# RWKV's Gram masks: ScalarE copies and GpSimd selects, or bitwise AND on VectorE

## Chip, cores and metric

One Trainium2 chip, one of its cores, one program. The metric is the device time of one execution in microseconds (us), the median over several runs. The engines are called PE (TensorE, matmuls), DVE (VectorE), ACT (ScalarE), POOL (GpSimd) and SP (SyncE, which issues most weight loads).

## The reference, cut to what matters

One block over 256 tokens of width 2048: a normed input is projected, four branches (HGRN2, S5, RWKV-7, Mamba-2) each make a 1024-wide output, and the gated outputs are projected up, summed, projected and added to the input. The change lies in the RWKV branch, whose recurrence over tokens is

```python
def step(state, inp):
    r_t, w_t, k_t, v_t, kk_t, a_t = inp
    sa = jnp.einsum('bhvk,bhk->bhv', state, -kk_t)
    state = (state * w_t[:, :, None, :]
             + sa[..., None] * (kk_t * a_t)[:, :, None, :]
             + v_t[..., None] * k_t[:, :, None, :])
    return state, jnp.einsum('bhvk,bhk->bhv', state, r_t)
```

for 16 heads of 64 channels. The kernel computes it in 4 chunks of 64 tokens. Within a chunk, the products of every pair of tokens are needed for each head: a 64 x 64 Gram matrix of (b, k) against (r, -kk), of which only the part with the later token on one side counts. For the r columns the diagonal belongs to it, for the kk columns it does not. The rest must be zero: these are the masks.

## The kernel before

**The stream.** The large matmuls (the input projection, the up projections, the output projection) are cut into chunks of 512 KB of weights. For each chunk SP loads `raw`; ACT copies it to `hi` in a rounded format (`split`, L207); DVE subtracts to get `lo` (L216); PE multiplies `hi` and `lo` with the activations (`pg`, L261). There are 3 `raw` and 4 `hi`/`lo` buffers.

**The jobs.** The branches are generators, started as jobs with priorities, that issue a stage of instructions and yield. A planner keeps a modelled clock for each engine (`t_pe`, `t_act`, `t_dve`, `t_sw` for POOL) from cost formulas in the helpers: `act` books 0.06 us + 0.87 ns an element, `tt` (two-tensor DVE operations) 0.06 us + 1.045 ns an element, `select` and `ld` book on `t_sw`. Between chunks `run_jobs` issues stages as long as neither `t_dve` nor `t_act` is more than 3 us ahead of `t_pe`. So booked costs decide where in each engine's queue a stage lands; each engine then runs its queue in order. The RWKV job is `c` (priority 1); the Mamba job `d0` starts after it, then `d1`, `a0`, `a1`; S5 tiles run beside them at lower priority.

**The Gram stage** is in `rwkv_branch`, for chunks c = 0 to 3. Two groups `i4` of four head pairs: 8 matmuls of `bk` with `L1` fill two PSUM banks `ps[0]`, `ps[1]` (one for each head of a pair, `e`), 128 partitions by 4 x 128. Of each bank one half of the partitions (`x`) goes to the tile `GB`, the other half (`y`) back into the unused half of the tile `L1[c][e]`: four ACT copies of 64 x 512 for each group (L207), 32 in all. When both groups are there, POOL clears what the mask forbids, in place, with four selects of 64 x 1024 (`select`, L275), and loads one half of `GB` to memory as `dab` (`ld`, L280). Four PSUM banks are shared by all jobs (`wait_banks`); the next group's products need banks that the copies have emptied. For c < 3 the transposes of `bk` follow, which ACT copies to `bkT`.

**After it**, `dab` is read back as `XA`, an inverse is computed on DVE in 31 dependent steps (`invtmp`, `XT`), loaded out and back (`dtt`, `TT`), and the four chunks are run in order with `L1`, `GB`, `TT` and `bkT` on PE. The branch ends in `oc`, which is multiplied with a gate `zs` into the tiles `o`, the operand of the up projection.

**Setup.** `setup_consts` makes constants on POOL in the first 20 us, the mask tile `lmask` (used elsewhere) among them, with selects at L365 and L367.

Traces call the tiles by name without their numbers, so `L` is `L1` and `pb` any of the four shared PSUM banks.

Of the kernel before, what the change touches and what calls it, by code (L numbers as in the profile page):

```python
# [11 lines left out]
F32 = mybir.dt.float32  # L12
F32R = mybir.dt.float32r
I8 = mybir.dt.int8
BF16 = mybir.dt.bfloat16
AF = mybir.ActivationFunctionType
ALU = mybir.AluOpType
# [296 lines left out]
def setup_consts(K):  # L314
    nc = K.nc
    d = K.d
    c = K.const
    K.pt = c.tile([128, NPAR], F32, name="pt")
    src = {"norm_pre": d["norm_pre"], "lb": d["hgrn_lb_logits"], "hgrn_norm": d["hgrn_norm"],
           "s5_d": d["s5_d"], "b_glu": d["s5_b_glu"], "w0": d["rwkv_w0"], "a0": d["rwkv_a0"],  # L320
           "k_k": d["rwkv_k_k"], "k_a": d["rwkv_k_a"], "r_k": d["rwkv_r_k"], "ln_w": d["rwkv_ln_w"],
           "ln_b": d["rwkv_ln_b"], "m2_norm": d["m2_norm"], "conv_b": d["m2_conv_b"],
           "mu": d["rwkv_mu"], "conv_w": d["m2_conv_w"], "a_re": d["s5_a_re"], "a_im": d["s5_a_im"]}
    rows = K.big([128, 3, 128], name="prow")
    nc.vector.memset(rows, 0.0)
    for m, n in enumerate(_PAR_ROWS):
        if m in (6, 12):
            yield
        o, r = PAR[n]
        a = src[n][0]  # L330
        if len(a.shape) == 2:
            a = a.rearrange("a b -> (a b)")
        K.ldx(rows[o % 128:o % 128 + r, o // 128, :], a.rearrange("(r p) -> r p", p=128))
    yield
    K.ones = c.tile([128, 1], F32, name="ones")
    nc.gpsimd.memset(K.ones, 1.0)
    K.halfpi = c.tile([128, 1], F32, name="halfpi")
    nc.gpsimd.memset(K.halfpi, HALF_PI)

    K.ind = c.tile([128, 2, 32], F32, name="ind")  # L340
    nc.gpsimd.memset(K.ind, 0.0)
    for e in range(2):
        for g in range(2):
            nc.gpsimd.memset(K.ind[64 * e:64 * e + 64, g, 2 * g + e:2 * g + e + 1], 1.0)
    K.m64 = c.tile([128, 512], BF16, name="m64")
    nc.gpsimd.memset(K.m64, 1.0)
    nc.gpsimd.memset(K.m64[:, 0:512:64], 0.0)
    K.m256 = c.tile([128, 512], BF16, name="m256")
    nc.gpsimd.memset(K.m256, 1.0)
    nc.gpsimd.memset(K.m256[:, 0:512:256], 0.0)  # L350
    K.causal = c.tile([128, 128], F32, name="causal")
    nc.gpsimd.memset(K.causal, 1.0)
    nc.gpsimd.affine_select(out=K.causal, in_=K.causal, pattern=[[1, 128]], base=0, channel_multiplier=-1,
                            compare_op=ALU.is_ge, fill=0.0)

    K.lmask = c.tile([128, 7, 64], I8, name="lmask")
    nc.gpsimd.memset(K.lmask, 0.0)
    for e in range(2):
        x = slice(64 * e, 64 * e + 64)
        for lv in range(6):  # L360
            h = 1 << lv
            nb = 32 // h
            v = K.lmask[x, lv + 1, :].rearrange("p (b u) -> p b u", u=2 * h)[:, :, h:2 * h]
            nc.gpsimd.memset(v, 1.0)
            nc.gpsimd.affine_select(out=v, in_=v, pattern=[[-2 * h, nb], [0, h]], base=0, channel_multiplier=1,  # L365
                                    compare_op=ALU.is_ge, fill=0.0)
            nc.gpsimd.affine_select(out=v, in_=v, pattern=[[2 * h, nb], [0, h]], base=h - 1, channel_multiplier=-1,  # L367
                                    compare_op=ALU.is_ge, fill=0.0)
    K.omu = c.tile([128, 25], F32, name="omu")
    yield  # L370
    for e in range(2):
        x = slice(64 * e, 64 * e + 64)
        nc.vector.tensor_copy(out=K.lmask[x, 0, :], in_=K.ident[x, x])
    yield from K.wait_banks(1)
    ps = K.bank()
    for j in range(3):
        K.tr(ps[:, j * 128:(j + 1) * 128], rows[:, j, :])
    nc.vector.tensor_copy(out=K.pt, in_=ps[:, 0:NPAR])
    K.ts(K.omu, K.parv("mu"), -1.0, 1.0, ALU.mult, ALU.add)
# [16 lines left out]
def rwkv_branch(K, rw):  # L396

    nc = K.nc
# [10 lines left out]
    for g in range(2):  # L409
# [3 lines left out]
        for ii in range(4):  # L413
            i = 4 * g + ii
# [3 lines left out]
        for ii in range(4):  # L418
            i = 4 * g + ii
# [23 lines left out]
    ps = K.bank()  # L443
# [34 lines left out]
    ps = K.bank()  # L478
# [4 lines left out]
    b = ic  # L483
# [10 lines left out]
    L1 = [[K.big([128, 8, 2, 64], name=f"L1{c}{e}") for e in range(2)] for c in range(4)]  # L494
    for c in range(4):
        o = c % 2
        s0, s1 = 64 * c, 64 * c + 64
        for e in range(2):
            x = slice(64 * e, 64 * e + 64)
# [12 lines left out]
    for c in range(4):  # L512
# [3 lines left out]
        for e in range(2):  # L516
            x = slice(64 * e, 64 * e + 64)
# [9 lines left out]
    GB, bkT = [], []  # L527
# [3 lines left out]
    for c in range(4):  # L531
        o = c % 2
        GB.append(K.big([128, 8, 2, 64], name=f"GB{c}"))
        bkT.append(K.big([128, 16, 64], name=f"bkT{c}") if c < 3 else None)
        for i4 in range(2):
            yield from K.wait_banks(2)
            ps = [K.bank([128, 4, 128]) for _ in range(2)]
            for ii in range(4):
                i = 4 * i4 + ii
                for e in range(2):  # L540
                    x = slice(64 * e, 64 * e + 64)
                    K.mm(ps[e][:, ii, :], fl2(bk[c][x, i]), fl2(L1[c][e][x, i]))
            yield 1
            for e in range(2):
                x = slice(64 * e, 64 * e + 64)
                y = slice(64 * (1 - e), 64 * (1 - e) + 64)
                i0 = slice(4 * i4, 4 * i4 + 4)
                K.act(L1[c][e][y, i0].rearrange("p i a b -> p i (a b)"), ps[e][y], AF.Copy)
                K.act(GB[c][x, i0].rearrange("p i a b -> p i (a b)"), ps[e][x], AF.Copy)
                if e == 0:  # L550
                    yield 0
            del ps
            if i4 == 0:
                yield 0
        pat = [[0, 8], [-1 if o == 0 else 1, 2], [1, 64]]
        base = 0 if o == 0 else -1
        for e in range(2):
            x = slice(64 * e, 64 * e + 64)
            y = slice(64 * (1 - e), 64 * (1 - e) + 64)
            for ap in (GB[c][x], L1[c][e][y]):  # L560
                K.select(ap, pattern=pat, base=base, channel_multiplier=-1, compare_op=ALU.is_ge, fill=0.0)
            K.ld(dab[c, :, e, :, :].rearrange("i s t -> s i t"), GB[c][x, :, 1 - o, :])
        if c == 3:
            bk[c] = None
            break

        pt = []
        yield from K.wait_banks(2)
        for e in range(2):
            x = slice(64 * e, 64 * e + 64)  # L570
            ps = K.bank([128, 8, 64])
            pt.append(ps)
            for i in range(8):
                K.tr(ps[:, i, :], fl2(bk[c][x, i]), 64 * e)
        yield 1
        for e in range(2):
            K.act(bkT[c][:, e:16:2, :], pt[e], AF.Copy)
        bk[c] = None
        del pt, ps
        yield 0  # L580
# [10 lines left out]
    for s in range(31):  # L591
        n, m = s + 1, 31 - s
# [29 lines left out]
    for q in range(2):  # L622
        ps = [K.bank([128, 8, 32]) for _ in range(2)]
        zps.append(ps)
        for o in range(2):
            z0 = 64 * (1 - o) + 32
            for h in range(16):
                i, e = h // 2, h % 2
                x = slice(64 * e, 64 * e + 32)
# [12 lines left out]
    for q in range(2):  # L642
        ps = K.bank([128, 16, 32])
# [44 lines left out]
    for q in range(2):  # L688
# [4 lines left out]
        else:  # L693
            for e in range(2):
                x = slice(64 * e, 64 * e + 64)
# [6 lines left out]
        for o in range(2):  # L702
            c = 2 * q + o
# [4 lines left out]
            for h in range(16):  # L708
                i, e = h // 2, h % 2
# [11 lines left out]
            for h in range(16):  # L721
                i, e = h // 2, h % 2
                K.mm(pu[64 * e:64 * e + 64, i, :], TT[q][ab:ab + 64, h, :], R1(e)[:, i, :])
            yield 1
            for e in range(2):
                x = slice(64 * e, 64 * e + 64)
# [3 lines left out]
            if c < 3:  # L730
                yield from K.wait_banks(1)
                pst = K.bank([128, 8, 64])
                for h in range(16):
                    i, e = h // 2, h % 2
                    K.mm(pst[64 * e:64 * e + 64, i, :], bkT[c][:, h, :], wc[e][:, i, 1, :])
            for h in range(16):
                i, e = h // 2, h % 2
                x = slice(64 * e, 64 * e + 64)
# [3 lines left out]
            if c < 3:  # L742
                if o == 1:
                    carry = GB[0][:, :, 0, :]
                for e in range(2):
                    x = slice(64 * e, 64 * e + 64)
# [16 lines left out]
    v = K.fm("v")  # L763
# [3 lines left out]
    for q in range(2):  # L767
        y = Y[q]
# [15 lines left out]
        for g in range(2):  # L784
            yield from K.wait_banks(1)
            ps = K.bank([128, 4, 128])
            for ii in range(4):
                i = 4 * g + ii
                K.tr(ps[:, ii, :], yf[:, i * 128:(i + 1) * 128])
            yield 1  # L790
            for ii in range(4):
                i = 4 * g + ii
# [1018 lines left out]
def hybrid_block_kernel(ctx: ExitStack, tc: tile.TileContext, *args):  # L1811
# [311 lines left out]
    for key, c, f0 in (("k", C_K, 8), ("r", C_R, 0), ("v", C_V, 16)):  # L2123
        for j in range(4):
            def then(key=key):
                rw[key + "_done"] = True
                if key == "k":
                    S.start("c", rwkv_branch(K, rw), 1)
            add(_Unit("fm", w_in, KT, c + 256 * j, 256, hmv,
                      shift_done("rv" if key == "v" else lazy(rw, key, lambda key=key: K.fm(key)), 2 * j, f0 + 2 * j, 2,  # L2130
                                 then if j == 3 else None)))
# [91 lines left out]
    K.ident = K.const.tile([128, 128], F32, name="ident")  # L2223
    make_identity(nc, K.ident)
    consts = setup_consts(K)
    next(consts)
    next(pro)
# [70 lines left out]
```

## Time and profile before

| what | us |
|---|---|
| median of 3 runs | 1437.47 (1435.5 to 1440.03) |
| the profiled execution | 1429.66 |
| its span, first to last instruction | 1427.6 |
| PE busy | 1392.8 |
| DVE busy | 1039.6 |
| ACT busy | 823.4 |
| POOL busy | 159.8 |

Busy time counts each engine's own instructions inside the span; engines work side by side, so the times don't add. A row of a timeline reads: start, duration, engine, line of the helper that recorded the instruction, operation, output tile and input tiles, shape, count; in brackets how long the engine stood idle before it and what ended that. A row of groups reads: line, engine, operation, tiles, shapes, count | busy us, mean ns of one | idle us before them and what ended it.

### The profile page before, as it was taken

The page shows a single profiled execution, that of the slowest core. Times are in us where ns is not written, and L with a number is a line of the kernel's source. Part 1 is how long each engine was busy: PE and PEld are TensorE (multiplying, and loading weights), DVE is VectorE, ACT ScalarE, POOL GpSimd, SP SyncE. Part 2 cuts the span into 40 slices and gives each one's busy share as a digit, 9 for nine tenths or more (in the row PEclk, how much of TensorE's full clock was granted, in tenths as well). Part 3 has the DMA queues.
Part 4 walks back from the last instruction along what each step waited for, and adds up shares of the span by engine and source line. Part 5 has one row for each costly group of instructions (what it writes and reads, how often), then busy time and mean ns, then how long its engine had stood idle before and what let it go on. Part 6 is the DMA issues. An engine that isn't in the chain of part 4 may idle for free.

```text
span 1427.6 us, 24650 instructions
## 1 busy us (share of the span) xinstructions
PE 1392.8 (98%) x9751; PEld 1226.1 (86%) x9751; DVE 1039.6 (73%) x1422; ACT 823.4 (58%) x1132; POOL 159.8 (11%) x268
## 2 busy tenths in 40 slices
PE   8998999989999999899999999999999999999997
PEld 8998998989999878898887888888789887888886
DVE  6785976778946767498985689667978778576655
ACT  6465445666437574665557874778656444544442
POOL 6012004133030102011000001000010100000000
PEclk9999999999999999999999999999999999999999
DMA  7776778857795858897565669556586866686564
GB/s 214 226 222 187 213 214 244 221 148 204 233 246 162 216 176 172 254 220 248 171 216 175 187 193 226 188 178 196 172 203 192 216 182 194 205 267 194 184 193 137
DMA packets 199040, 288.62 MB, mean 202 GB/s; under 512 B 12453, under 2 KB 116750, under 8 KB 198926
## 3 DMA queue, kind: packets, MB, share of 16 engines
q1 hardware_dynamic: 169614, 237.15, 55.0%
q0 software_dynamic: 25216, 43.05, 14.6%
q10 hardware_dynamic: 4096, 6.86, 1.4%
q8 instruction: 76, 1.25, 0.4%
q14 instruction: 38, 0.31, 0.1%
HBM read 268.33 MB, written 18.66 MB: 201 GB/s over the span
## 4 chain that ended last, share of the span: by engine, by line
PE 69%; DMA 10%; DVE 9%; ACT 8%; issue 3%; ACTq 0%; SPq 0%; DVEq 0%
PE pg L261 63%; DMA raw<-in_w_in_dram 9%; PE pb L261 6%; DVE lo L216 4%; ACT hi L207 3%; PE pb L267 1%; ACT L207 1%; DVE ev L229 1%; DVE invtmp L216 1%; DVE tb L243 1%; DMA x<-in_x_dram 1%; DVE XT L216 0%; DVE ta L216 0%; ACT hT L207 0%; ACT sw L207 0%
## 5 line engine op out<-in xcount | busy, mean ns | idle before, releaser
L216 DVE TENSOR_TENSOR lo<-raw,hi 128x1024 fp32r<-128x1024 f32 x444 | 541.1, 1223 | 345.6 <-ACT hi L207 342.8
L207 ACT ACTIVATE hi<-raw 128x1024 fp32r<-128x1024 f32 x444 | 465.8, 1054 | 526.3 <-PE pg L261 291.0
L261 PE MATMUL pg<-h,hi 128*128 128x256 f32 x2624 | 482.4, 287 | 8.1 <-ACT hi L207 7.7
L261 PE MATMUL pg<-hi,h 128*128 128x512 f32 x1408 | 448.8, 393 | 0.0
L261 PEld LDWEIGHTS pg<-h,hi 128*128 128x128 f32 x2624 | 411.3, 193 | 13.7 <-ACT hi L207 8.5
L261 PE MATMUL pg<-h,lo 128*128 128x256 f32 x1312 | 372.5, 286 | 2.9 <-DVE lo L216 2.4
L261 PEld LDWEIGHTS pg<-hi,h 128*128 128x128 f32 x1408 | 264.3, 188 | 59.2 <-issue 3.3
L261 PE MATMUL pg<-lo,h 128*128 128x512 f32 x704 | 274.8, 390 | 0.1
L261 PEld LDWEIGHTS pg<-h,lo 128*128 128x128 f32 x1312 | 252.0, 193 | 4.6 <-DVE lo L216 3.3
L261 PE MATMUL pg<-hi,o 128*128 128x512 f32 x512 | 162.7, 392 | 0.0
L261 PEld LDWEIGHTS pg<-lo,h 128*128 128x128 f32 x704 | 132.3, 188 | 27.1 <-DVE lo L216 1.3
L261 PEld LDWEIGHTS pg<-hi,o 128*128 128x128 f32 x512 | 96.1, 188 | 21.1 <-issue 0.4
L261 PE MATMUL pg<-lo,o 128*128 128x512 f32 x256 | 99.8, 390 | 0.0
L261 PE MATMUL pg<-hi,mhl 128*128 128x512 f32 x224 | 71.1, 391 | 0.0
L280 POOL DMA_DIRECT2D gb<-in_gate_bias_dram x16 | 8.7, 545 | 527.5 <-DVE gate L216 527.5
L207 ACT ACT_TABLE_LOAD x48 | 61.6, 1283 | 6.3 <-DVE mss L235 3.2
L261 PEld LDWEIGHTS pg<-lo,o 128*128 128x128 f32 x256 | 48.1, 188 | 9.5
L261 PEld LDWEIGHTS pg<-hi,mhl 128*128 128x128 f32 x224 | 42.0, 188 | 8.7
L261 PE MATMUL pg<-lo,mhl 128*128 128x512 f32 x112 | 43.6, 389 | 0.0
L243 DVE TENSOR_TENSOR_SCAN tb<-s5p,ta 128x256 f32<-128x256 f32 x64 | 43.0, 716 | 0.2
L280 POOL DMA_DIRECT2D us<-duhl x16 | 10.3, 646 | 135.6 <-PE pb L261 96.9
L261 PEld LDWEIGHTS pg<-lo,mhl 128*128 128x128 f32 x112 | 21.0, 188 | 4.3
(371 smaller groups left out, 1375.9 us busy)
## 6 DMA issues: line engine op xcount, KB each, us to landing
raw<-in_w_in_dram SPq DMA_DIRECT2D x340, 512.0 KB
raw<-in_w_up_dram SPq DMA_DIRECT2D x64, 512.0 KB
raw<-in_w_out_dram SPq DMA_DIRECT2D x32, 512.0 KB
us<-duhl POOLq DMA_DIRECT2D x16, 256.0 KB, 7.2
bs<-ds5b POOLq DMA_DIRECT2D x16, 256.0 KB, 8.3
gb<-in_gate_bias_dram POOLq DMA_DIRECT2D x16, 256.0 KB, 5.0
raw<-in_s_w_glu_dram SPq DMA_DIRECT2D x8, 512.0 KB
x<-in_x_dram SPq DMA_DIRECT2D x4, 512.0 KB
```

The lines of the kernel that those rows point to most:

```text
L207: return self.nc.scalar.activation(out=out, in_=in_, func=func, **kw)
L216: return self.nc.vector.tensor_tensor(out=out, in0=in0, in1=in1, op=op)
L229: return self.nc.vector.scalar_tensor_tensor(out=out, in0=in0, scalar=scalar, in1=in1, op0=op0, op1=op1, **kw)
L243: return self.nc.vector.tensor_tensor_scan(out=out, data0=data0, data1=data1, initial=0.0, op0=ALU.mult, op1=ALU.add)
L261: return self.nc.tensor.matmul(out, lhsT, rhs, start=start, stop=stop, **kw)
L267: return self.nc.tensor.transpose(out, in_, self.ident[b:b + p, b:b + p])
L280: return self.nc.gpsimd.dma_start(out=out, in_=in_)
```

## The change

A constant tile `gmask`, 128 x 3 x 64 of 32-bit integers, is made once on POOL: all bits set where the mask allows, zero elsewhere (rows 0 and 2 without the diagonal, row 1 with it). A slice of two neighbouring rows is the mask of a chunk, in the order that the chunk's parity `o` needs. In the Gram stage the four ACT copies of each group become four DVE bitwise ANDs, which read PSUM and the mask as integers and write `L1` and `GB`. The 16 selects on POOL go; the `dab` loads stay.

```diff
+    K.gmask = c.tile([128, 3, 64], I32, name="gmask")
+    nc.gpsimd.memset(K.gmask, -1)
+    for e in range(2):
+        for n in range(3):
+            v = K.gmask[64 * e:64 * e + 64, n, :]
+            nc.gpsimd.affine_select(out=v, in_=v, pattern=[[1, 64]], base=-1 if n != 1 else 0, channel_multiplier=-1,
                                     compare_op=ALU.is_ge, fill=0.0)
...
                 i0 = slice(4 * i4, 4 * i4 + 4)
-                K.act(L1[c][e][y, i0].rearrange("p i a b -> p i (a b)"), ps[e][y], AF.Copy)
-                K.act(GB[c][x, i0].rearrange("p i a b -> p i (a b)"), ps[e][x], AF.Copy)
+                keep = lambda z: K.gmask[z, 1 - o:3 - o, :].unsqueeze(1).to_broadcast([64, 4, 2, 64])
+                for out, z in ((L1[c][e], y), (GB[c], x)):
+                    K.tt(out[z, i0].bitcast(I32), ps[e][z].rearrange("p i (a b) -> p i a b", a=2).bitcast(I32), keep(z),
+                         ALU.bitwise_and)
                 if e == 0:
                     yield 0
...
-        pat = [[0, 8], [-1 if o == 0 else 1, 2], [1, 64]]
-        base = 0 if o == 0 else -1
         for e in range(2):
             x = slice(64 * e, 64 * e + 64)
-            y = slice(64 * (1 - e), 64 * (1 - e) + 64)
-            for ap in (GB[c][x], L1[c][e][y]):
-                K.select(ap, pattern=pat, base=base, channel_multiplier=-1, compare_op=ALU.is_ge, fill=0.0)
             K.ld(dab[c, :, e, :, :].rearrange("i s t -> s i t"), GB[c][x, :, 1 - o, :])
```

More of the change, by code (lines that the diff above doesn't have):

```diff
@@ L14 @@
 I8 = mybir.dt.int8
+I32 = mybir.dt.int32
 BF16 = mybir.dt.bfloat16
@@ L368, in setup_consts @@
                                     compare_op=ALU.is_ge, fill=0.0)
+    K.gmask = c.tile([128, 3, 64], I32, name="gmask")
[4 more added lines that the diff above has]
+            nc.gpsimd.affine_select(out=v, in_=v, pattern=[[1, 64]], base=-1 if n != 1 else 0, channel_multiplier=-1,
+                                    compare_op=ALU.is_ge, fill=0.0)
     K.omu = c.tile([128, 25], F32, name="omu")
```

## The prediction

> **What bounds the kernel now.** I read the page's head first, for the engine that has no room.
>
> ```profile
> span 1427.6 us, 24650 instructions
> PE 1392.8 (98%) x9751; PEld 1226.1 (86%) x9751; DVE 1039.6 (73%) x1422; ACT 823.4 (58%) x1132; POOL 159.8 (11%) x268
> ```
>
> TensorE (PE) has work for 1392.8 of 1427.6 us. The edit touches none of that work, so it can gain only from the 35 us in which PE stands still, or lose by adding to them. The second view is the busy time by stretches of 20 us; columns: stretch, its length, busy us (instructions) of PE, weight load, DVE, ACT, POOL, then granted clock, DMA share, GB/s. The Gram stage lies between 230 and 335 us.
>
> ```profile
> 280.00:300.00 20.00, 18.00 (x167) 17.00 (x165) 9.06 (x12) 16.03 (x26) 6.50 (x7) 1.00 0.97 213
> 300.00:320.00 20.00, 17.09 (x157) 16.05 (x156) 19.12 (x22) 11.12 (x16) 7.26 (x6) 1.00 0.39 113
> 320.00:340.00 20.00, 18.97 (x171) 18.14 (x172) 16.15 (x20) 14.70 (x24) 9.36 (x10) 1.00 0.63 181
> 360.00:380.00 20.00, 20.00 (x169) 20.00 (x168) 19.06 (x34) 9.46 (x10) 0.00 (x0) 1.00 0.85 250
> 560.00:580.00 20.00, 16.36 (x71) 13.44 (x70) 6.66 (x8) 3.18 (x3) 3.96 (x7) 0.90 1.27 277
> 580.00:600.00 20.00, 19.57 (x153) 19.30 (x152) 10.95 (x13) 16.77 (x23) 2.48 (x3) 0.93 0.75 215
> ```
>
> Three things are to be seen. In the first three stretches PE idles 2.00 + 2.91 + 1.03 = 5.9 us. By 360 us the stage's successor (a serial inverse) fills DVE to 95% and PE still does not wait. And far later, at 560, PE loses 3.6 us and then clock. The third view, PE's own timeline, names each idle of the Gram stage (in brackets: idle before, and what ended it).
>
> ```profile
> 286.76 0.71 PE L267 MATMUL pb<-ident,bk 64*128 64x64 f32 x8 [1.72 <-ACT GB L207]
> 297.67 0.99 PE L261 MATMUL pb<-us,bs 128*128 128x256 f32 x4 [0.29 <-ACT bkT L207]
> 301.98 0.48 PE L261 MATMUL pb<-L,bk 64*128 64x128 f32 x2 [0.45 <-ACT GB L207]
> 303.07 1.16 PE L261 MATMUL pb<-L,bk 64*128 64x128 f32 x14 [0.60 <-ACT GB L207]
> 321.03 0.41 PE L261 MATMUL pb<-ta,cu 128*32 128x256 f32 x2 [2.89 <-ACT bkT L207]
> ```
>
> They add to 5.95 us: 2.77 us (1.72 + 0.45 + 0.60) wait for exactly the ACT copies that the change removes (PSUM banks come free late), 3.18 us for another ACT copy, bkT.
>
> **The change part by part.** First the groups that it removes, from the groups of 230 to 336 us (count | busy, mean ns).
>
> ```profile
> L207 ACT ACTIVATE GB<-pb 64x512 f32<-64x512 f32 x16 | 9.5, 592 | 0.2
> L207 ACT ACTIVATE L<-pb 64x512 f32<-64x512 f32 x16 | 9.4, 587 | 0.6 <-ACT ev L207 0.4
> L275 POOL TENSOR_SCALAR_AFFINE_SELECT L<-L 64x1024 f32<-64x1024 f32 x8 | 10.8, 1346 | 0.5
> L275 POOL TENSOR_SCALAR_AFFINE_SELECT GB<-GB 64x1024 f32<-64x1024 f32 x8 | 9.8, 1219 | 35.2 <-ACT GB L207 35.2
> ```
>
> *Removed:* ACT loses 32 copies, 9.5 + 9.4 = 18.9 us; POOL loses 16 selects, 10.8 + 9.8 = 20.6 us. *Added:* 32 DVE operations, 64 partitions by 512 elements, one input from PSUM, one from SBUF. No bitwise operation is in the trace; the nearest rows are a float tensor_tensor out of PSUM and one that writes alternate halves of the partitions.
>
> ```profile
> 301.88 0.68 DVE L216 TENSOR_TENSOR ta<-pb,cs 128x512 f32<-128x512 f32 x1
> 302.48 0.68 DVE L216 TENSOR_TENSOR tb<-pb,cs 128x512 f32<-128x512 f32 x1
> 91.42 1.38 DVE L216 TENSOR_TENSOR bx<-tb 64x512 f32<-64x512 f32 x2
> ```
>
> Neighbours on all partitions start 0.60 us apart; the bx pair (each half writes other partitions, neither needs the other) takes 1.38 us, 0.69 each. The masks alternate halves in the same way, so I take 0.69: 32 x 0.69 = 22.1 us of DVE. Bounds: 32 x 0.60 = 19.2 below; above, twice the row, 44 us, should 32-bit integers run slower (no row speaks for it). [...]
>
> *Given back on DVE:* while POOL runs its selects, DVE's neighbours stretch. Groups over the whole run first, then the same forms inside 230 to 336 us, and two undisturbed single rows.
>
> ```profile
> L216 DVE TENSOR_TENSOR lo<-raw,hi 128x1024 fp32r<-128x1024 f32 x444 | 541.1, 1223 | 345.6 <-ACT hi L207 342.8
> L243 DVE TENSOR_TENSOR_SCAN tb<-s5p,ta 128x256 f32<-128x256 f32 x64 | 43.0, 716 | 0.2
> L216 DVE TENSOR_TENSOR lo<-raw,hi 128x1024 fp32r<-128x1024 f32 x27 | 35.8, 1334 | 25.0 <-ACT hi L207 25.0
> L243 DVE TENSOR_TENSOR_SCAN tb<-s5p,ta 128x256 f32<-128x256 f32 x4 | 5.2, 1348 | 0.0
> L229 DVE SCALAR_TENSOR_TENSOR ph<-ph 128x512 f32<-128x512 f32 x2 | 2.7, 1370 | 0.1
> L234 DVE TENSOR_SCALAR ph<-ph 128x512 f32<-128x512 f32 x2 | 1.8, 887 | 0.0
> 295.82 0.41 DVE L234 TENSOR_SCALAR ph<-ph 128x512 f32<-128x512 f32 x1
> 296.26 0.69 DVE L229 SCALAR_TENSOR_TENSOR ph<-ph 128x512 f32<-128x512 f32 x1
> ```
>
> 27 x (1.334 - 1.223) = 3.0; scans 5.2 - 4 x 0.67 = 2.5 (0.67 is 43.0 / 64); ph 2.7 - 2 x 0.69 = 1.3 and 1.8 - 2 x 0.41 = 1.0. Together 7.8 us that leave with the selects. DVE's net load: 22.1 - 7.8 = +14.3 us.
>
> *What of it is on PE's path.* The three waits for Gram copies: at 286.76 and 302 ACT is late because its own queue is full, and DVE idles just then:
>
> ```profile
> 283.20 1.22 DVE L216 TENSOR_TENSOR lo<-raw,hi 128x1024 fp32r<-128x1024 f32 x1 [4.06 <-ACT hi L207]
> 288.91 1.33 DVE L216 TENSOR_TENSOR lo<-raw,hi 128x1024 fp32r<-128x1024 f32 x1 [4.49 <-ACT hi L207]
> 300.74 1.23 DVE L216 TENSOR_TENSOR lo<-raw,hi 128x1024 fp32r<-128x1024 f32 x1 [2.65 <-ACT hi L207]
> ```
>
> Four masks (2.8 us) fit each of these gaps, so I take the 2.77 us as gained. The 2.89 us at 321.03: bkT sits on ACT behind a Silu that waits for DVE.
>
> ```profile
> 319.34 0.63 ACT L207 ACTIVATE ev<-ev 128x512 f32<-128x512 f32 x1 [3.48 <-DVE ev L229]
> 320.38 1.09 ACT L207 ACTIVATE bkT<-pb 128x512 f32<-128x512 f32 x2 [0.40 <-ACT ev L207]
> ```
>
> DVE ran without a gap from 300.74 until then, and two of its rows there are stretched ones.
>
> ```profile
> 305.72 3.02 DVE L243 TENSOR_TENSOR_SCAN tb<-s5p,ta 128x256 f32<-128x256 f32 x2
> 308.67 2.44 DVE L216 TENSOR_TENSOR lo<-raw,hi 128x1024 fp32r<-128x1024 f32 x1
> ```
>
> The four scans of the group lie there (2.5 us of stretch) and this lo (2.44 - 1.22 = 1.2), so DVE sheds 3.7 us before the Silu and takes on 2.8 us (four masks, the others lie in the gap before) to 5.5 us (all eight). This wait moves by -0.9 to +1.8; I take -0.9, since that gap is there. What is queued behind a mask on DVE is the next lo, for which PE waits; lo has the four-chunk lead of the hi/lo buffers. Sum: -2.8 - 0.9 = -3.7 us, plus 0.3 for one new wait of PE for a mask (half of 0.69): **-3.4 us**.
>
> *Setup:* one POOL memset and six selects of 64 columns early on, at the 0.48 us of the small selects, some 3.2 us. POOL then stands idle before the next thing anyone waits for:
>
> ```profile
> L365 POOL TENSOR_SCALAR_AFFINE_SELECT lmask<-lmask 64x32 int8<-64x32 int8 x12 | 5.7, 476 | 0.8
> 34.78 1.43 POOL L280 DMA_DIRECT2D duhl<-uhl  x2 [11.05 <-ACT uhl L207]
> ```
>
> That 11.05 us hides it; without this cover it would cost up to 3.2 us.
>
> *Moved:* the eight dab transfers stay on POOL's queue but follow DVE masks instead of selects, and the later loads queued there (S5 tiles, XA) with them. After the last chunk POOL runs four selects (4 x 1.28, the mean of the two groups, = 5.1 us) before XA can be loaded; that falls away, 5 us for the RWKV chain. *The planner* books 0.595 us of DVE for each mask where it booked 0.505 of ACT (from its formulas), so it hands out background stages in another order from 233 us on. That is not to be read from this trace; it is noise of either sign, bounded by one DMA collision like the one at 560 (below).
>
> **The rivals.** *Slower: RWKV arrives late.* The branch is a chain through DVE, and its product must be ready when PE reaches the up projection:
>
> ```profile
> 640.12 0.68 DVE L216 TENSOR_TENSOR o<-zs,o 128x512 fp32r<-128x512 f32 x1
> 655.32 0.39 PE L261 MATMUL pg<-hi,o 128*128 128x512 f32 x1
> ```
>
> Slack 655.32 - 640.80 = 14.5 us; forecast delay 14.3 - 5 = 9.3, hidden. If nothing is given back and XA gains nothing, the delay is 22.1 and PE stalls 7.6; a stall of that length also costs clock, as the collision at 573 shows:
>
> ```profile
> 576.31 0.80 PE L261 MATMUL pg<-h,hi 128*128 128x256 f32 x2 [3.17 <-ACT hi L207]
> ```
>
> After 3.17 us of idle the stretches above grant 0.90 and 0.93: 20 x 0.10 + 20 x 0.07 = 3.4 us lost besides. The slow case: -3.4 + 7.6 + 3.4 = +7.6, 1445. It decides from 14.5 us of delay. [...]
>
> *Faster: all Gram waits go and the collision with them.* -5.95 us if bkT is never late; if the new order also moves the late RWKV loads off PE's raw weights, 3.17 + 3.4 more: -12.5, 1425. For it: ACT's 41.9 us of the 60 between 280 and 340 lose three chunks' copies, 14.2 us. Against it: those loads come whatever the masks do.
>
> *No change: the wait moves house.* PE waits for masks behind DVE's lo and convolution work as it waited for copies; 0 to +2, 1437 to 1439. DVE at 19.12 of 20 in 300 to 320 speaks for it, its gaps at 283 to 300 against.
>
> **How the numbers follow.** The profiled execution took 1429.66 us (span 1427.6 and 2.1 around it), 7.8 below the median 1437.47 of the runs (1435.5 to 1440.03); I apply the sum to the median: 1437.5 - 3.4 = 1434. Within 0.3% (4.3 us) a measurement of this kernel can't be told from no change. Chances: the forecast (-1 to -5.95, its own range 1431.5 to 1436.5) 0.40, of which 0.14 beyond -4.3; faster rival 0.26; wait moved 0.14; slow rival 0.20 (a little of "moved" beyond +4.3 included). Faster 0.14 + 0.26 = 0.40, same 0.26 + 0.12 = 0.38, slower 0.22. The range runs from the faster rival's end to the slow case, 1425 to 1446, with a tenth outside on each side.
>
> **What the changed profile would show.** Right: ACT near 804, POOL near 142, DVE near 1054 us; 32 masks of 0.68 to 0.69; lo back at 1223 ns in the stage and no stretched scans; no PE wait for Gram copies; oc's product still ready before PE's first up projection. Wrong: masks over 0.8 us, PE waits ended by a DVE mask, a stall before the up projection, or a fourth half-clock stretch.

## Result and the profile after

| kernel | us, median (range) | ratio to before, 95% interval |
|---|---|---|
| before | 1436.49 (1434.54 to 1440.03) | |
| changed | 1446.55 (1445.85 to 1449.51) | 1.0071 [1.0046, 1.0096] |

The change makes the kernel slower, by 10 us or 0.7%. The profiled execution of the changed kernel took 1446.5 us, its median; that of before lay 7 us under its own. The two profiles therefore differ by 17.2 us of span, and a single difference between them is not yet part of the 10.

The head of the changed kernel's page:

```profile
span 1444.8 us, 24629 instructions
PE 1399.4 (97%) x9751; PEld 1228.7 (85%) x9751; DVE 1052.1 (73%) x1454; ACT 808.1 (56%) x1104; POOL 141.6 (10%) x259
```

The engines moved as forecast (ACT near 804, POOL near 142, DVE near 1054). PE's span minus its busy time was 34.8 us and is 45.4. The groups of DVE between 230 and 345 us (count | busy, mean ns):

```profile
L217 DVE TENSOR_TENSOR GB<-pb,gmask 64x512 int32<-64x512 int32 x16 | 11.0, 689 | 0.2
L217 DVE TENSOR_TENSOR L<-pb,gmask 64x512 int32<-64x512 int32 x16 | 10.9, 684 | 0.2
L217 DVE TENSOR_TENSOR lo<-raw,hi 128x1024 fp32r<-128x1024 f32 x31 | 37.6, 1219 | 16.9 <-ACT hi L208 16.7
L244 DVE TENSOR_TENSOR_SCAN tb<-s5p,ta 128x256 f32<-128x256 f32 x4 | 2.5, 677 | 0.0
```

A mask takes 0.69 us, and the 32 durations add to 21.9 us (forecast 22.1); lo is back at 1219 ns and the scans at 677. The stretches that the prediction showed, and three much later ones (columns as there):

```profile
280.00:300.00 20.00, 17.72 (x171) 16.68 (x170) 14.70 (x24) 10.02 (x15) 5.07 (x8) 0.99 1.25 257
300.00:320.00 20.00, 19.90 (x169) 18.90 (x169) 19.65 (x28) 8.51 (x12) 1.38 (x2) 0.92 0.45 129
320.00:340.00 20.00, 20.00 (x182) 19.16 (x181) 18.97 (x30) 9.34 (x12) 2.50 (x4) 1.00 0.64 183
660.00:680.00 20.00, 19.28 (x85) 15.36 (x83) 14.81 (x30) 7.64 (x8) 7.77 (x12) 1.00 1.22 239
680.00:700.00 20.00, 15.06 (x120) 11.49 (x121) 12.94 (x14) 8.37 (x10) 0.00 (x0) 0.83 0.64 211
700.00:720.00 20.00, 18.98 (x95) 15.85 (x94) 16.75 (x26) 10.64 (x12) 1.11 (x2) 1.00 0.61 184
```

Between 280 and 340 us PE idles 2.28 + 0.10 + 0 = 2.4 us instead of 5.9, but it loses 0.2 + 1.6 us of clock where before lost none. Whether the masks did this is asked in experiment 2. And from 660 to 720 PE idles 0.72 + 4.94 + 1.02 = 6.7 us and loses 20 x 0.17 = 3.4 of clock, 10.1 together. Before had nothing of it there (from 700 to 720 its PE is busy throughout, too):

```profile
660.00:680.00 20.00, 20.00 (x155) 15.87 (x154) 15.59 (x24) 12.57 (x15) 3.25 (x5) 1.00 0.89 279
680.00:700.00 20.00, 20.00 (x101) 16.90 (x100) 17.29 (x24) 8.98 (x12) 0.00 (x0) 1.00 0.44 141
```

The loss is not made up afterwards. Counted along the weight stream, the 193rd of the 444 `lo` operations starts 1.9 us later than in before (661.20 against 659.33), the 209th 13.1 us later (723.78 against 710.69).

No mask runs at 660. PE's own timeline of the changed kernel names what it waits for there, and ACT's names what is late:

```profile
680.51 1.13 PE L262 MATMUL pb<-xst,cbt 128*128 128x256 f32 x4 [1.22 <-DVE xst L217]
685.51 1.15 PE L262 MATMUL pb<-xd,dk 128*64 128x64 f32 x32 [1.12 <-DVE dk L217]
689.98 1.97 PE L262 MATMUL pb<-xd,dk 128*64 128x64 f32 x32 [3.32 <-DVE dk L217]
```

```profile
677.53 1.06 ACT L208 ACTIVATE hi<-raw 128x1024 fp32r<-128x1024 f32 x1 [4.85 <-DMA raw<-in_w_in_dram]
```

PE waits for tiles of another branch (Mamba's `xst`, `dk`), and the weights `raw`, which are PE's other work, come late by DMA: from 650 to 705 us ACT waits for them 4.79 + 4.85 + 3.41 + 1.18 = 14.2 us, in before 3.17 + 2.04 = 5.2. What the DMAs collide with is seen in POOL's timeline, whose queue issues the loads of all background branches, first of the changed kernel, then of before:

```profile
661.06 0.56 POOL L281 DMA_DIRECT2D gb<-in_gate_bias_dram  x1 [67.42 <-DVE gate L217]
661.61 0.63 POOL L281 DMA_DIRECT2D us<-duhl  x1
...
665.32 0.60 POOL L281 DMA_DIRECT2D mx<-dx  x1
...
675.95 0.89 POOL L281 DMA_DIRECT2D dk<-dacs  x1 [1.82 <-DVE merged L230]
```

```profile
631.24 0.64 POOL L280 DMA_DIRECT2D us<-duhl  x1 [37.36 <-DVE bb L216]
638.98 0.58 POOL L280 DMA_DIRECT2D cu<-du  x1
659.26 0.54 POOL L280 DMA_DIRECT2D gb<-in_gate_bias_dram  x1 [19.71 <-DVE gate L216]
```

`gb` is the bias of a gate unit, a 128 x 512 load that `gate_unit` issues on POOL at the unit's first chunk. Its buffer is free only when DVE has done an earlier gate's add, so this load stands at the head of POOL's queue until then: 67.42 us in the changed kernel. Before, the loads of the next S5 tile (`us`, `bs`, `cu`) stood ahead of it and were out by 640; now they stand behind it and start with Mamba's (`mx` to `dk`), eleven loads in one burst from 661 to 677, against the weights. Nothing in the masks asks for this order. It comes from the planner, which hands out background stages by the time booked on each engine.

### The profile page after: what moved, and what is told of

Same layout as the page of the kernel before. It is cut to its first block, busy times and chain, and to the rows that moved or that the text cites. A ratio compares the mean times of both kernels' runs of the same rounds, so it can differ in the third digit from the quotient of the medians.

```text
span 1444.8 us, 24629 instructions
## 1 busy us (share of the span) xinstructions
PE 1399.4 (97%) x9751; PEld 1228.7 (85%) x9751; DVE 1052.1 (73%) x1454; ACT 808.1 (56%) x1104; POOL 141.6 (10%) x259
## 4 chain that ended last, share of the span: by engine, by line
PE 59%; DMA 14%; DVE 12%; ACT 8%; issue 6%; ACTq 0%; SPq 0%; DVEq 0%
PE pg L262 53%; DMA raw<-in_w_in_dram 13%; DVE lo L217 5%; PE pb L262 5%; ACT hi L208 4%; DMA raw<-in_w_up_dram 1%; DVE ta L217 1%; PE pb L268 1%; ACT L208 1%; DVE tb L244 1%; DVE tb L217 1%; DVE E L217 1%; DMA x<-in_x_dram 1%; ACT cs L208 1%; ACT hT L208 0%
## 5 line engine op out<-in xcount | busy, mean ns | idle before, releaser
L208 ACT ACTIVATE hi<-raw 128x1024 fp32r<-128x1024 f32 x444 | 465.1, 1054 | 558.0 <-PE pg L262 252.6
L262 PE MATMUL pg<-ghl,hi 128*128 128x256 f32 x128 | 23.1, 283 | 0.0
```

The costliest lines, as they stand in the source:

```text
L208: return self.nc.scalar.activation(out=out, in_=in_, func=func, **kw)
L262: return self.nc.tensor.matmul(out, lhsT, rhs, start=start, stop=stop, **kw)
```

## The experiments

Three theories. **Order**: the engines gained what the prediction said, and the planner's new order, with a load at the wrong place in POOL's queue, cost more. **Load**: DVE's 14 us more made RWKV or Mamba late, whatever the order. **Setup**: `gmask`'s selects delay the start. The diffs are shortened.

**1. The change's instructions, the old plan.** The masks run on DVE, but ACT and POOL are booked as before, so that PE's order is that of before.

```diff
-K.tt(out[z, i0].bitcast(I32), ps[e][z]..., keep(z), ALU.bitwise_and)
+K.book("t_act", 0.06 + K._n(o3) * 0.87e-3, o3, [ps[e][z]])
+nc.vector.tensor_tensor(out=..., in0=..., in1=keep(z), op=ALU.bitwise_and)
...
+for ap in (GB[c][x], L1[c][e][y]):
+    K.book("t_sw", 0.07 + K._n(ap) * 1.05e-3, ap, (ap,))
```

> The changed kernel's instructions (32 masks on DVE, no selects on POOL, the mask's setup), but the planner is told the old costs (0.505 us of ACT for each mask, 1.145 us of POOL for each select that is no longer there), so PE's queue holds the same order as in the kernel before. Theory A (the loss comes from the new order of the background stages, the engines' own work gains): the Gram waits for copies go (2.8 us) and the S5 loads stay ahead of the gate-bias load on POOL, so 1430 to 1437 us, no half-clock stretch near 690 us. Theory B (the extra 13 us of DVE work, or a late RWKV branch, makes the loss): still 1442 to 1450 us.

Measured: 1434.06 us, ratio 0.9976 [0.996, 0.9991], -3.4 us by the ratio. With the old order the new instructions are a small gain, in total of the size forecast; load and setup, both still in, do not make it slower. From 660 to 720 PE neither idles nor loses clock, and the two `lo` operations named above both start 3.8 us later than in before, so nothing is lost between them.

**2. The old instructions, the new plan.** Copies on ACT and selects on POOL, booked as the changed kernel books; PE's order is that of the changed kernel.

```diff
-K.act(L1[c][e][y, i0]..., ps[e][y], AF.Copy)
+K._dve(out[z, i0], (ps[e][z],), K._n(out[z, i0]) * 1.045)
+nc.scalar.activation(out=o3, in_=ps[e][z], func=AF.Copy)
...
-K.select(ap, ...)
+nc.gpsimd.affine_select(out=ap, in_=ap, ...)
```

> The kernel before, with its ACT copies and POOL selects, but the planner is told the changed kernel's costs (0.595 us of DVE for each copy, nothing for the selects), so PE's queue holds the order of the changed kernel. Theory A (order): 1443 to 1452 us, with PE idle and at half clock between 660 and 710 us. Theory B (DVE work): 1434 to 1440 us, as before.

Measured: 1447.02 us, 1.0066 [1.0045, 1.0087], +9.5. Without one mask the order alone costs what the change costs. (The two halves don't add up exactly, -3.4 + 9.5 against +10.2; the intervals leave room for it.) POOL's timeline and the stretches of this run show the same place, with the S5 loads starting at 659.00 right behind the gate bias:

```profile
658.45 0.56 POOL L280 DMA_DIRECT2D gb<-in_gate_bias_dram  x1 [66.92 <-DVE gate L216]
```

```profile
660.00:680.00 20.00, 19.08 (x84) 15.30 (x83) 14.17 (x29) 8.53 (x8) 6.24 (x10) 1.00 1.27 272
680.00:700.00 20.00, 16.54 (x139) 13.21 (x138) 14.90 (x17) 9.06 (x13) 0.00 (x0) 0.91 0.58 181
```

This run also answers the question of the Gram stage:

```profile
300.00:320.00 20.00, 17.32 (x149) 16.47 (x146) 15.84 (x19) 13.47 (x21) 6.29 (x6) 0.91 0.43 125
```

Those 2.7 us are all its idle time from 280 to 340, with the copies still on ACT and the selects on POOL; the changed kernel idles 2.4 there, and both lose 1.8 us of clock. So with the new order the idle time falls there with or without the masks.

**3. Late setup.** The changed kernel, with `gmask` made at the start of `rwkv_branch` and no longer in `setup_consts`.

```diff
 def setup_consts:
-    nc.gpsimd.memset(K.gmask, -1)    # and the six selects
 def rwkv_branch:
+    nc.gpsimd.memset(K.gmask, -1)    # and the six selects
```

> The changed kernel with one thing moved: the memset and the six selects that make the mask are issued when the RWKV branch starts, not in the first 20 us. Theory C (the setup on POOL delays the start, where PE idles 1.2 us more between 20 and 40 us): the first 40 us lose no more than before, 1443 to 1446 us, 1 to 3 us under the changed kernel. Theories A and B: within 1 us of the changed kernel, 1446.

Measured: 1445.2 us, 1.0043 [1.0021, 1.0065]. Still slower: setup is not the main cause. A gain of 1 us can't be told from none here, so the two expectations are not separated.

**4. Another order of before.** The planner's lead `AHEAD`, 3.0 to 3.3, in the kernel before: a different order of everything, with no mask.

```diff
-AHEAD = 3.0
+AHEAD = 3.3
```

> The kernel before, with none of the change, and the planner's limit (how far ACT and DVE may be booked ahead of PE) at 3.3 instead of 3.0 us: an order of the background stages that is as arbitrary as the changed kernel's. If an order drawn at random costs or gains several us by itself (theory A in its general form): more than 4 us away from 1436.5, to either side. If the order before is robust: 1434 to 1440 us.

Measured: 1439.16 us, 1.0013 [0.9994, 1.0031]. Here the S5 loads stay ahead of the gate bias at 665 us, the fourth of the 16. A new order as such need not cost 10 us; this one does.

**5. and 6. The bookings one by one.** The changed kernel's instructions, with masks booked on DVE and the vanished selects still booked on POOL; then masks booked on ACT and selects not booked.

```diff
 # 5: added to the changed kernel
+K.book("t_sw", 0.07 + K._n(ap) * 1.05e-3, ap, (ap,))    # for each vanished select
 # 6: in the changed kernel, for each mask
+K.book("t_act", 0.06 + K._n(o3) * 0.87e-3, o3, [ps[e][z]])    # in place of DVE's booking
```

> The changed kernel's instructions, masks booked on DVE as in the change, but the planner still books the 16 selects on POOL (1.145 us each) that are no longer there. POOL's queue then holds an S5 tile's loads ahead of the third gate-bias load, as in the kernel before. Theory A1 (that place in POOL's queue is what costs): 1431 to 1438 us, no loss between 660 and 710 us. Rival (booking the masks on DVE by itself makes a bad order): 1442 to 1450 us.

> The other half: the changed kernel's instructions, masks booked as ACT copies as before, the selects not booked on POOL. POOL's queue then holds the gate-bias load ahead of the S5 tile's loads, as in the changed kernel. Theory A1: 1442 to 1448 us, with the loss between 660 and 710 us. Rival (the booking on DVE makes the bad order): 1431 to 1438 us.

Measured: 1437.37 and 1451.36 us, the second slower than its expectation allowed (1442 to 1448). With the changed kernel and experiment 1 in the table (ratios to before; the instructions are the same in all four):

| masks booked on | selects still booked on POOL | not booked |
|---|---|---|
| ACT | 0.9976 [0.996, 0.9991] | 1.0104 [1.0088, 1.012] |
| DVE | 1.0002 [0.9987, 1.0017] | 1.0071 [1.0046, 1.0096] |

Both kernels of the right column are slower, neither of the left: what costs is that the planner no longer sees 18 us of POOL (16 bookings of 0.07 + 1024 x 0.00105). Booking the masks on DVE instead of ACT is not what makes the loss: it costs 0.3% in one column and gains 0.3% in the other. In POOL's timeline with the selects booked (first two rows, masks on DVE) the S5 load goes out at 614 and the fourth gate bias (the expectation calls it the third) waits 24.59 us with those loads ahead of it; without (last row, masks on ACT) it waits 68.40:

```profile
614.04 0.65 POOL L281 DMA_DIRECT2D us<-duhl  x1
665.57 0.54 POOL L281 DMA_DIRECT2D gb<-in_gate_bias_dram  x1 [24.59 <-DVE gate L217]
```

```profile
670.03 0.56 POOL L281 DMA_DIRECT2D gb<-in_gate_bias_dram  x1 [68.40 <-DVE gate L217]
```

**7. and 8. The gate bias off POOL's queue.** In the changed kernel, then in before, the 16 loads go to SP's queue at the unit's fifth chunk. The booking stays.

```diff
-if c == 0: u.pre()
+if c == 4: u.pre()
...
-K.ldx(gb, src)
+K.book_dma("t_sw", 1.2, gb, src); nc.sync.dma_start(out=gb, in_=src)
```

> The changed kernel; only the 16 gate-bias loads move, from POOL's queue at a gate unit's first chunk to SP's queue at its fifth chunk, with the planner's booking kept, so PE's, DVE's and ACT's queues are as in the changed kernel. Theory A1 (the gate-bias load in front of the S5 tile's and Mamba's loads holds them on POOL until 661 us, then ten start in 15 us and the weights come late): the S5 loads start near 640 us, apart from the others, PE loses 2 us or less between 660 and 710 us instead of 10, and the time is 1436 to 1441 us. Rival A2 (the loss there comes from the order of Mamba's stages in PE's queue, whatever the loads do): still 1444 to 1449 us.

> The kernel before with the same move of the gate-bias loads to SP, as the control of the run ahead. Theory A1: nothing was held up there at a cost, so within 3 us of before, 1434 to 1440. If the move is worth something for itself: below 1434.

Measured: the changed kernel 1426.61 us, 0.9923 [0.9901, 0.9945]; before 1427.27 us, 0.993 [0.9913, 0.9948]. The edit is worth some 20 us to the one and 10 to the other, and the 10 us between them are gone. The first lies 9 us under the range expected, because the edit does more than cure the loss at 660, as the control shows. PE works through the changed kernel's order in the first of them, so the rival that Mamba's place in PE's queue makes the loss is out. POOL and the stretch of the changed kernel with it:

```profile
640.82 0.64 POOL L281 DMA_DIRECT2D us<-duhl  x1 [52.86 <-DVE oc L217]
```

```profile
660.00:680.00 20.00, 19.23 (x85) 15.64 (x84) 20.00 (x35) 10.55 (x11) 1.79 (x2) 1.00 0.77 248
680.00:700.00 20.00, 18.98 (x162) 15.44 (x161) 13.41 (x18) 11.19 (x15) 0.56 (x1) 1.00 0.57 178
```

The loads from `us` to `mbc` are spread over 640 to 656, the DMA share falls from 1.22 to 0.77 and no clock is lost. In before the same edit clears the collision at 560 that the prediction saw (PE 16.36 of 20 there). First POOL's row in before, then the stretch with the edit:

```profile
552.65 0.54 POOL L280 DMA_DIRECT2D gb<-in_gate_bias_dram  x1 [82.30 <-DVE gate L216]
560.00:580.00 20.00, 19.46 (x123) 15.15 (x122) 15.68 (x18) 10.57 (x13) 1.59 (x3) 1.00 0.67 212
```

So the collision at 560 was of the same kind: a gate bias stood 82.30 us at the head of POOL's queue, and 15 loads behind it started from 553 to 572. With the edit the S5 loads among them go out at 510 to 521.

**9. The moment or the queue.** Experiment 7 changed both. Here the loads come at the fifth chunk but stay on POOL.

```diff
-if c == 0: u.pre()
+if c == 4: u.pre()    # K.ldx(gb, src) stays on POOL
```

> The changed kernel with the gate-bias loads issued at the unit's fifth chunk, as in the experiment that moved them, but left on POOL's queue; bookings and the order of PE, DVE and ACT are those of that experiment. That experiment changed two things at once, the queue and the moment; this one changes the moment alone. Theory of the blocked queue: what costs is the place in POOL's queue. Four chunks later than before, the load still stands ahead of the S5 tile's loads (us, bs, cu) and still waits for the gate add of the gate before last, which is some 67 us away, so the S5 loads still start only after about 655 us in one burst, PE loses 5 to 10 us between 660 and 720, and the time is that of the changed kernel: 1443 to 1449 us, ratio 1.004 to 1.009. Rival, the moment: the gain came because the load was issued later, so less stood behind it while it waited; then the time falls to near that experiment's, 1426 to 1432 us, ratio 0.992 to 0.996, with the S5 loads spread over 640 to 655 and PE idle under 2.5 us from 660 to 720.

Measured: 1444.89 us, 1.0053 [1.0038, 1.0068]. What counts is the queue and not the moment; the S5 load starts at 665.81, right behind the gate bias:

```profile
665.26 0.56 POOL L281 DMA_DIRECT2D gb<-in_gate_bias_dram  x1 [66.89 <-DVE gate L217]
```

**10. to 12. Setup again, and all together.** With the gate bias off POOL: old plan and late setup; new plan and late setup; old plan and early setup. Each is made of the edits above.

> Masks on DVE with the old plan (as in the first run), the mask's setup at the start of the RWKV branch, and the gate-bias loads on SP. If the three effects add (masks -3.4, gate bias -10, setup -1 us): 1422 to 1425 us. If the gate-bias move already holds the others' gain: 1426 to 1428 us.

> The changed kernel and its plan, gate-bias loads on SP, and the mask's setup at the start of the RWKV branch. Against the same kernel with the early setup (1426.6): theory C (the early setup puts POOL's S5 weight loads into the first weight loads and PE waits 1.2 us): 1424 to 1426 us, and PE's idle time between 20 and 40 us back at 0.4. Without it: 1427.

> As the run with all three, but with the mask's setup in the first 20 us as in the change. Theory C: 1 to 2 us above it, with 1.5 us of PE idle between 20 and 40 us instead of 0.4. Without it: the same time.

| gate bias off POOL | early setup | late setup |
|---|---|---|
| old plan | 1423.39, 0.9913 [0.9896, 0.993] | 1422.31, 0.9905 [0.9888, 0.9922] |
| new plan | 1426.61, 0.9923 [0.9901, 0.9945] | 1430.07, 0.9943 [0.9924, 0.9963] |

Masks on DVE with the old plan and the bias off POOL are the best version, 1422.31 us, 14 us under before. With the queue unblocked the plan is worth 0.1% in one column and 0.4% in the other; with the gate bias on POOL and early setup it was 0.95% (0.9976 to 1.0071). The intervals of the second column don't overlap, so some effect of the order is left there, and these runs don't show where. The new plan with late setup missed its expectation (1424 to 1427). What setup is worth can't be read from them; it goes one way in one row and the other way in the next.

## Why the prediction was wrong

It forecast 1434 (1425 to 1446) and gave slower 0.22. The step that failed is the planner's order, put at nothing in the sum; it cost 9.5 us. By its own steps:

**The masks, 22.1 us, and 7.8 us given back: right** (groups above). But the durations, which add to 21.9 us, don't say how long the masks hold DVE: `ta` and `tb` last 0.68 each and start 0.60 apart. The starts tell. The first four masks write the upper, lower, lower and upper half of the partitions:

```profile
237.27 0.69 DVE L217 TENSOR_TENSOR L<-pb,gmask 64x512 int32<-64x512 int32 x1
237.98 0.68 DVE L217 TENSOR_TENSOR GB<-pb,gmask 64x512 int32<-64x512 int32 x1
238.59 0.67 DVE L217 TENSOR_TENSOR L<-pb,gmask 64x512 int32<-64x512 int32 x1
239.27 0.69 DVE L217 TENSOR_TENSOR GB<-pb,gmask 64x512 int32<-64x512 int32 x1
```

Where the half changes, the next mask starts 0.71 and 0.68 us later; where it stays, 0.61. In all eight groups of four the third mask starts 0.61 us behind the second. So one mask in four starts 0.61 us behind its predecessor, where the prediction took 0.69 for each, and 32 masks take DVE some 8 x 2.69 = 21.5 us (an estimate from this group).

**PE's Gram waits, -3.4 us: the total came by luck, as far as the runs show.** Experiment 1, which has the old order, measured -3.4, and idle time from 280 to 340 us fell by 5.9 - 2.4 = 3.5 us in the changed kernel. But the second came with the order (experiment 2), and the first is not found in the Gram stage, as follows. In the changed kernel one wait is left, still for bkT, and earlier; with the old order two for masks, larger than the 0.3 us that was allowed for. PE's timeline of the changed kernel, then of experiment 1:

```profile
298.41 1.16 PE L262 MATMUL pb<-L,bk 64*128 64x128 f32 x16 [2.28 <-ACT bkT L208]
```

```profile
303.72 0.46 PE L262 MATMUL pb<-L,bk 64*128 64x128 f32 x2 [1.93 <-DVE GB L561]
305.03 1.13 PE L262 MATMUL pb<-L,bk 64*128 64x128 f32 x14 [0.85 <-DVE GB L561]
```

So "Four masks (2.8 us) fit each of these gaps" failed at one chunk of experiment 1, whose stretches are:

```profile
280.00:300.00 20.00, 19.94 (x185) 19.07 (x184) 14.83 (x21) 13.58 (x22) 2.58 (x4) 1.00 1.16 245
300.00:320.00 20.00, 17.22 (x141) 16.56 (x141) 18.72 (x26) 6.04 (x7) 1.38 (x2) 0.91 0.33 89
320.00:340.00 20.00, 18.51 (x174) 17.34 (x173) 17.13 (x28) 10.16 (x16) 3.11 (x5) 1.00 0.61 178
```

Its idle there is 0.06 + 2.78 + 1.49 = 4.3 us, only 1.6 less than before, and the 0.91 costs 1.8 of clock. Together that is no gain in this stage, so where experiment 1's gain comes from stays open. With the new order no gain of the masks is to be seen: 1.0071 with them, 1.0066 without (experiment 2). The sum had no term for clock lost behind the waits that are left.

**Setup, hidden by 11.05 us: the cover was misread.** The prediction looked at the next POOL row with an idle time. But the `bri` loads stood behind the lmask selects, after `s5ld` and three short rows of `s5e`, with no idle time that could hide anything. Their issue moves 2.4 us (first row of each kernel), into the first weights, and PE waits in the changed kernel:

```profile
19.34 1.74 POOL L280 DMA_DIRECT2D bri<-in_s_b_re_dram  x1
29.40 1.06 ACT L207 ACTIVATE hi<-raw 128x1024 fp32r<-128x1024 f32 x1 [4.22 <-DMA raw<-in_w_in_dram]
20.00:40.00 20.00, 19.65 (x161) 19.13 (x160) 13.77 (x25) 10.66 (x17) 5.16 (x5) 1.00 0.85 198
```

```profile
21.73 1.74 POOL L281 DMA_DIRECT2D bri<-in_s_b_re_dram  x1
32.13 1.06 ACT L208 ACTIVATE hi<-raw 128x1024 fp32r<-128x1024 f32 x1 [5.75 <-DMA raw<-in_w_in_dram]
20.00:40.00 20.00, 18.43 (x153) 18.05 (x152) 12.77 (x23) 10.80 (x18) 7.36 (x9) 1.00 0.84 200
```

1.57 us of idle instead of 0.35; with late setup it is gone from the profiles (0.36 us in experiment 3). In the times it can't be told from nothing.

**The planner's order, "noise of either sign, bounded by one DMA collision like the one at 560": this is the step that failed.** It stood in the sum as zero. Measured alone (experiment 2) it is +9.5 us, more than the 3.17 + 3.4 of that collision. The prediction named the wrong bookings as its source: 0.595 us on DVE for 0.505 on ACT. It left out the 18 us of POOL bookings that go with the selects, and these decide (experiments 5 and 6). Which load would come first, and so the sign, could hardly be read from the trace. The danger could: the prediction priced the collision at 560 without asking what made it, and the answer is the `gb` row at 552.65, which waited 82.30 us at the head of POOL's queue. It looked at what is queued behind the masks on DVE, and of POOL's queue only at what follows the `dab` loads, not at the loads there that wait for something else.

**Slower rival, RWKV late, 1445: the right number for the wrong reason, by luck.** Its chain did come late, the slack shrank from 14.5 to 2.0 us (654.31 + 0.69 to 657.04), but PE did not stall there:

```profile
654.31 0.69 DVE L217 TENSOR_TENSOR o<-zs,o 128x512 fp32r<-128x512 f32 x1
657.04 0.48 PE L262 MATMUL pg<-hi,o 128*128 128x512 f32 x1
```

Experiment 1, with the same load on DVE, was faster, and there the slack is 15.0 us (644.06 to 659.08). So the chain came late by the order and not by the load, and the 9.3 us of delay that the prediction hid in the slack are not there. **Faster rival**: the collision can go, but by moving the gate bias and not by the masks. **The mark set for a wrong forecast, a fourth half-clock stretch, is met.** By stretches of 2 us, and apart from the end, before grants 0.50 in three places (from 136, 426 and 576 us), the changed kernel in four (from 140, 300, 434 and 690 us; from 680 to 700 it has 0.83 on the whole), and 0.53 and 0.55 in two more (at 250 and 588).

## What to carry to other kernels

Where a planner orders the work by booked costs, moving work between engines is two changes: what the engines do, and the order that the books produce; keep the old bookings once and measure the first alone. In a queue that issues loads in order, list every load that waits for something other than its predecessor, and how much stands behind it: here one small load that waited 67 or 82 us for its buffer had 11 or 15 behind it, which then started within 15 and 19 us. Put such loads on another queue: with them on SP's, though the weights follow there, the changed kernel took 0.9923 of before's time instead of 1.0071, and before 0.993 (experiments 7 and 8). How long they wait on SP's queue was not shown. A second buffer for the load, on POOL's queue, would be another way; no run tried it.

## What was not expected of the hardware

In these runs the length of a wait alone does not tell whether the clock falls. The changed kernel's 2.28 us wait, which ended at 298.41, was followed by half rate, 0.50 from 300 to 302 (stretches of 2 us):

```profile
298.00:300.00 2.00, 1.59 (x19) 1.47 (x20) 1.97 (x6) 1.79 (x3) 0.00 (x0) 0.92 0.32 65
300.00:302.00 2.00, 2.00 (x11) 2.00 (x11) 1.97 (x5) 0.82 (x2) 0.00 (x0) 0.50 0.65 212
```

Before's wait of 2.89 us, which ended at 321.03, kept its clock: 1.00 in every such stretch from 318 to 332. So 2.28 us was enough once, with PE busy for all 4 us from 292 to 296 before it. What decides between 2.28 and 2.89 these runs don't show.
